# One layer of a hybrid decoder on one core: the second head's keys and queries loaded into the place of the first rows

## The chip, the core and the metric

The kernel runs on one core of a Trainium2 chip: TensorE for matrix products, VectorE, ScalarE and GpSimd for the rest, SyncE as the queue that issues nearly all DMAs. The metric is device time in microseconds of one execution.

## What is computed

2048 prompt rows and 32 sample rows of 1024 numbers are normed, and one projection gives all head groups and the gate:

```
h = rmsnorm(x); p = h @ w_in
cb, cc, ch, q, k, v, mq, z = split(p)               # 3x256, 3x512, 256, 1024 columns
conv_y = cb * conv3(cc * ch)
for win, dil in ((128,1), (512,4), (2048,16)):      # 8 heads x 64, ALiBi, causal band per residue class
    o, lse = softmax_band(q, k, v, win, dil)
attn_o = merge(outs, lses)                          # weights by the softmax denominators
mem_o = softmax(mq @ mk^T) @ mv                     # 4 heads x 64, 256 memory tokens
x = x + (concat(conv_y, attn_o, mem_o) * silu(z)) @ w_out
y = rmsnorm(x)
```

The sample rows attend to 8 caches of 2048 keys. Outputs are y of both kinds of rows, the windows of k and v, the conv buffer and the memory keys and values, all in float32.

## The kernel before, in words

**Rows and projections.** Products run with operands split into a high and a low part, three products each (`mm3`, L354). The normed rows lie column-wise in `hT`: half "A" (`hA_hi`, `hA_lo`) holds the first 1024 prompt rows and the 32 sample rows, half "B" the others. `proj_steps` (L383) takes one tile of 128 weight columns through column groups of rows: 384, 384 and 288 of A, 512 and 512 of B (`GROUPS`); each group is 24 matmuls into one PSUM bank, which is then evicted.

**z.** z has eight column tiles. `ev_z` (L680) applies SiLU on ScalarE into one of two buffers `ehi` and spills it to the DRAM tensor `dz` (`spill`, L374 to L377); prompt and sample columns of the last group of A are two spills. The last two tiles (`ZL` is 2) are projected for half B at their place, and for half A in `z_last` (L697), which `interleave` (L1104) mixes with the score products of head 0. Then the room of the rows is given up: `p0.close()`.

**Heads.** Eight attention heads, then four memory heads, are `units`. Odd units take their tiles from `vals[1]` and `keys[1]`, even ones from `vals[0]` and `keys[0]`. `load_qk` (L802 to L808) issues six DMAs of 512 KB by SyncE: high and low part of k into `ks`, and of q twice each into `qh` and `ql`. `regroup` (L823) copies `ks` into `kr` in another order, four copies on ScalarE for dilation 16 and later four for dilation 4. `scores` runs the products `qk` (L791, L792): those of dilation 16 by `kr`, those of dilation 1 by `ks`, those of dilation 4 by `kr`. `values` subtracts a running maximum (`Rm`, fetched through the DRAM tensor `dmax`, L747 and L748) on GpSimd, takes the exponential on ScalarE (L924, L925 for `S`, L929 for `S3`, L945 for `SS`), and multiplies with `v` (L917).

**What sets the order.** Head 1's pools lie in the room of the rows, so they are opened after `z_last`, and `units[1].load_qk()` (L1107) and its `regroup` come next. From then on `periods` (L1123) runs: the scores of unit n beside the values of unit n - 1, with the loads of unit n + 1 in it (`loads`, L1110); TensorE and SyncE keep the order in which the code issues there (`manual_schedule`), the other engines are ordered by a scheduler by priorities. Every engine works its own list in order. SyncE's DMAs use eight completion counters in turn, `DMAHW0` to `DMAHW7`; a DMA waits for the one before it on its counter. After the last memory head's scores the room of the keys is given up, and W_out is loaded in eight chunks, split into `woh` and `wol` in the pool `wo` (L1138 to L1152).

Of the kernel before, what the change touches and what calls it, by code (L numbers as in the profile page):

```python
# [9 lines left out]
R = mybir.dt.float32r  # L10
# [8 lines left out]
D = 1024  # L19
T = 2048  # L20
# [5 lines left out]
ZL = 2  # L26
# [248 lines left out]
def tile_step(ctx, tc, x_prompt, x_sample, mem_prompt, ck, cv, cconv, cmk, cmv, g_in, w_in, conv_w,  # L275
# [87 lines left out]
    NA = T // 2 + NS  # L363
    GROUPS = [("A", 0, 384), ("A", 384, 384), ("A", 768, 288), ("B", 0, 512), ("B", 512, 512)]
    hT = {}

    def split_cols(half, o, n):

        if half == "B":
            return [(0, 1024 + o, n)]  # L370
        if o + n <= 1024:
            return [(0, o, n)]
        return [(0, o, 1024 - o), (1024 - o, T, NS)]
# [9 lines left out]
    def proj_steps(src, c0, evac, halves, lo_eng, keep=None):  # L383

        wh, wl = keep.get(c0) or load_w(src, c0, lo_eng) if keep is not None else load_w(src, c0, lo_eng)
        if keep is not None:
            keep[c0] = wh, wl
        for half, o, n in GROUPS:
            if half not in halves:
                continue  # L390
            hh, hl = hT[half]
            ps = psP.tile([128, 512], F, name="pp")
            mm3(ps[:, :n], lambda d: wh[:, d], lambda d: wl[:, d], lambda d: hh[:, d, o:o + n], lambda d: hl[:, d, o:o + n])
            evac(ps[:, :n], half, o, n)
            yield

    xr = x_prompt[0].rearrange("(b r) d -> r b d", r=16)
# [15 lines left out]
    hA = p0.enter_context(tc.tile_pool(name="rowsA", bufs=1))  # L413
    wp = p0.enter_context(tc.tile_pool(name="weights", bufs=2))
    hT["A"] = [hA.tile([128, 8, NA], R, name="hA_" + s) for s in ("hi", "lo")]
    with ExitStack() as p1:
        hB = p1.enter_context(tc.tile_pool(name="rowsB", bufs=1, side="right"))
        hT["B"] = [hB.tile([128, 8, 1024], R, name="hB_" + s) for s in ("hi", "lo")]
        with ExitStack() as pv:
# [41 lines left out]
            def rows(rb):  # L461
# [3 lines left out]
                norm_t((xr[rb] if rb else None) if rb < 16 else xs, n, gt, hT[half], c0)  # L465
                return half, c0

            def values(rb, half, c0):
                if rb == 16:
                    c0 = NA - 128  # L470
                hh, hl = hT[half]
                ps = psP.tile([128, 512], F, name="pp")
                mm3(ps, lambda d: hh[:, d, c0:c0 + 128], lambda d: hl[:, d, c0:c0 + 128], lambda d: wvh[:, d], lambda d: wvl[:, d])
# [223 lines left out]
    def z_last():  # L697
        for ct in range(8 - ZL, 8):
            yield from z_proj(ct, "A")
# [8 lines left out]
    keys[0] = p2q.enter_context(tc.tile_pool(name="keys0", bufs=1, side="right", reuse_waits="tile"))  # L708

# [397 lines left out]
    keys[1] = p2q.enter_context(tc.tile_pool(name="keys1", bufs=1, reuse_waits="tile"))  # L1107
    units[1].load_qk()
# [31 lines left out]
    woh, wol = {}, {}  # L1140
    for d in reversed(CH):
        woh[d] = wo.tile([128, D], R, name="woh%d" % d)
        wol[d] = wo.tile([128, D], R, name="wol%d" % d)
# [151 lines left out]
```

## Time and profile before

| | |
|---|---|
| median of the timed runs | 1369.4 us (1365.25 to 1371.61, 3 runs) |
| profiled execution | 1372.67 us, span 1370.6 us |
| TensorE busy | 1241.9 us (91%), mean granted clock 0.961 |
| VectorE, ScalarE, GpSimd busy | 643.0, 436.6, 458.9 us |
| DMA | 229.56 MB, mean 167 GB/s |

The profiled execution's own time is the span, first to last instruction, and 2 us around it. Times below count from the span's start. The idle time of an engine is put down to what ended it; an instruction's own row shows it in brackets.

### The profile page before, as it was taken

Reading aid. Unit: us, or ns where it says so; the run is one execution under the profiler, and the core shown is the slowest. Engines: PE = TensorE matmul, PEld = TensorE weight load, DVE = VectorE, ACT = ScalarE, POOL = GpSimd, SP = SyncE. Lnnn points to the kernel's source line nnn. Section 1 sums busy time; section 2 is a strip of 40 time slices with the busy share of each in tenths; the row PEclk is TensorE's granted clock in tenths of the full one; section 3 lists DMA queues with packets and bytes.
Section 4 is the critical chain, followed back from the end, with each engine's and each line's share of the span. In section 5 each row is a group of like instructions: output and inputs, shape, how many; then the busy total and the mean of one; then the engine's idle time right before and its main releaser. Section 6 shows DMA issues by size and latency. Waiting matters only on the chain. (4 is left out here: it accounts for less than half of the span.)

```text
span 1370.6 us, 20158 instructions
## 1 busy us (share of the span) xinstructions
PE 1241.9 (91%) x7814; PEld 1000.6 (73%) x7814; DVE 643.0 (47%) x1201; ACT 436.6 (32%) x692; POOL 458.9 (33%) x398
## 2 busy tenths in 40 slices
PE   6999999988899999999999938889889877999997
PEld 5778898977788777778887936666667442678886
DVE  4555121466556612301640437777777235554442
ACT  5433032223232010011122225556665465421111
POOL 3120010355556201101640014666666565110000
PEclk9999999999999999999999969999999989999999
DMA  6453142477887246575546357888887846876641
GB/s 230 131 154 104 41 145 87 169 260 244 268 259 253 74 96 160 158 190 176 162 151 157 86 123 169 173 183 186 185 185 164 204 112 186 240 218 202 190 155 70
DMA packets 228102, 229.56 MB, mean 167 GB/s; under 512 B 67348, under 2 KB 182280, under 8 KB 223912
## 3 DMA queue, kind: packets, MB, share of 16 engines
q1 hardware_dynamic: 216488, 207.30, 55.9%
q10 hardware_dynamic: 11520, 20.98, 4.1%
q8 instruction: 62, 1.02, 0.3%
q14 instruction: 32, 0.26, 0.1%
HBM read 171.92 MB, written 56.31 MB: 167 GB/s over the span
## 5 line engine op out<-in xcount | busy, mean ns | idle before, releaser
L359 PE MATMUL b<-hA_hi,whi 128*128 128x384 f32 (+1 forms) x576 | 191.4, 332 | 13.7 <-ACT big L607 11.4
L359 PE MATMUL b<-hA_hi,wlo 128*128 128x384 f32 (+1 forms) x576 | 189.0, 328 | 0.0
L359 PE MATMUL b<-hA_lo,whi 128*128 128x384 f32 (+1 forms) x576 | 188.6, 327 | 0.0
L351 POOL TENSOR_TENSOR wlo<-wraw,whi 128x512 fp32r<-128x512 f32 x56 | 80.9, 1461 | 295.5 <-ACT whi L350 294.8
L359 PE MATMUL b<-hB_hi,whi 128*128 128x512 f32 (+1 forms) x416 | 164.1, 394 | 9.7 <-ACT big L607 2.0
L124 POOL TENSOR_TENSOR spr<-sk,sqb 128x512 f32<-128x512 f32 (+2 forms) x110 | 121.7, 1117 | 127.1 <-DMA sqb<-dqs 43.3
L359 PE MATMUL b<-hB_lo,whi 128*128 128x512 f32 (+1 forms) x416 | 163.1, 392 | 0.0
L359 PE MATMUL b<-hB_hi,wlo 128*128 128x512 f32 (+1 forms) x416 | 162.8, 391 | 0.0
L359 PEld LDWEIGHTS b<-hA_hi,whi 128*128 128x128 f32 x576 | 110.2, 191 | 20.0 <-ACT big L607 12.3
L125 DVE TENSOR_REDUCE sc<-spr 128x8 f32<-128x512 f32 (+1 forms) x160 | 88.4, 572 | 73.7 <-POOL spr L124 73.3
L795 DVE SCALAR_TENSOR_TENSOR S<-dt,b 128x128 f32<-128x128 f32 (+2 forms) x224 | 70.1, 355 | 103.6 <-PE b L792 69.7
L359 PEld LDWEIGHTS b<-hA_hi,wlo 128*128 128x128 f32 x576 | 110.1, 191 | 4.1 <-issue 3.3
L359 PEld LDWEIGHTS b<-hA_lo,whi 128*128 128x128 f32 x576 | 110.0, 191 | 2.9 <-issue 2.9
L1198 PE MATMUL b<-woh,mh 128*128 128x512 f32 x256 | 99.9, 393 | 5.0 <-DVE xo L1228 3.3
L409 POOL TENSOR_TENSOR ss<-ss,nhalf 128x1 f32<-128x1 f32 (+1 forms) x34 | 20.8, 613 | 243.9 <-DVE ss L408 235.0
L1198 PE MATMUL b<-woh,ml 128*128 128x512 f32 x256 | 100.4, 394 | 0.2 <-DVE ml L1190 0.2
L359 PEld LDWEIGHTS b<-hB_hi,whi 128*128 128x128 f32 x416 | 79.2, 190 | 28.1 <-issue 3.2
L1198 PE MATMUL b<-wol,mh 128*128 128x512 f32 x256 | 98.7, 389 | 0.0
L928 POOL TENSOR_TENSOR S<-S,Rm 128x512 f32<-128x512 f32 x32 | 40.3, 1281 | 170.3 <-DMA Rm<-dmax 146.4
L828 ACT ACTIVATE kr<-ks 128x512 fp32r<-128x512 f32 x64 | 69.0, 1117 | 79.8 <-PE b L792 63.8
L791 PE MATMUL b<-qh,kr 128*128 128x256 f32 x256 | 75.1, 323 | 21.4 <-DMA qh<-dq_hi 20.9
L359 PEld LDWEIGHTS b<-hB_lo,whi 128*128 128x128 f32 x416 | 79.2, 190 | 19.8 <-issue 3.3
(234 smaller groups left out, 2370.1 us busy)
## 6 DMA issues: line engine op xcount, KB each, us to landing
sk<-in_cache_win_k_dram SPq DMA_DIRECT2D x72, 256.0 KB, 4.1
vq<-in_cache_win_v_dram SPq DMA_DIRECT2D x36, 512.0 KB, 4.1
wraw<-in_w_in_dram SPq DMA_DIRECT2D x48, 256.0 KB, 3.7
sqb<-dqs SPq DMA_DIRECT2D x48, 256.0 KB, 4.3
qh<-dq_hi SPq DMA_DIRECT2D x24, 512.0 KB, 10.4
ql<-dq_lo SPq DMA_DIRECT2D x24, 512.0 KB, 10.6
Rm<-dmax SPq DMA_DIRECT2D x24, 512.0 KB, 4.4
v<-out_dram SPq DMA_DIRECT2D x16, 512.0 KB, 17.8
```

The costliest lines, as they stand in the source:

```text
L124: E.tensor_mul(pr[:n, :width], kt, qt)
L125: nc.vector.tensor_reduce(dst, pr[:n, :width].rearrange("p (h e) -> p h e", e=64), axis=AX.X, op=OP.add)
L351: lo_eng.tensor_sub(lo[:, a:a + 4], raw, f32(hi[:, a:a + 4]))
L359: nc.tensor.matmul(ps, a(d), b(d), start=(n == 0), stop=(n == 23))
L409: nc.gpsimd.tensor_tensor(ss[:n], ss[:n], nhalf[:n], op=OP.pow)
L791: nc.tensor.matmul(out, keys, a, start=True, stop=False)
L795: nc.vector.scalar_tensor_tensor(S, dt, sl, ps, op0=OP.mult, op1=OP.add)
L828: nc.scalar.activation(self.kr[:, r4 * 512:(r4 + 1) * 512].rearrange("p (a b) -> p a b", a=d // 4), src[:, r4], AF.Copy)
L928: nc.gpsimd.tensor_sub(S3[:, r4], S3[:, r4], mr[:, r4])
L1198: nc.tensor.matmul(self.ps[k], l[:, d], r[d][:, sl], start=first and i == 0, stop=last and i == 2)
```

## The change

Three things, all about half A's first group of 384 rows.

1. Half A is held in three tiles, one for each column group: `hA0`, `hA1`, `hA2`, each with both parts. `hA0` keeps its room to the end of the kernel; the two others are given up with the rest of the rows.
2. `z_last` goes by column group: the first group of both tiles of z, then the second of both, then the third. After the first group of both it calls `units[1].load_qk()`.
3. `ks`, `qh` and `ql` of all odd units are three parts of `hA0` (3 x 2048 = 2 x 8 x 384 elements of a partition). Only `kr` and the partial maxima come from the pool `keys1`, opened after `z_last` as before. At the end, chunks 0 to 2 of `woh` and `wol` lie in `hA0`.

```diff
--- before.py
+++ after.py
@@ -364,6 +364,13 @@
     GROUPS = [("A", 0, 384), ("A", 384, 384), ("A", 768, 288), ("B", 0, 512), ("B", 512, 512)]
     hT = {}
 
+    def rows_at(half, o):
+
+        if half == "B":
+            return hT["B"], o
+        g = min(o // 384, 2)
+        return (hT["A"][g][:, 0], hT["A"][g][:, 1]), o - 384 * g
+
     def split_cols(half, o, n):
 
         if half == "B":
@@ -388,9 +395,9 @@
         for half, o, n in GROUPS:
             if half not in halves:
                 continue
-            hh, hl = hT[half]
+            (hh, hl), p = rows_at(half, o)
             ps = psP.tile([128, 512], F, name="pp")
-            mm3(ps[:, :n], lambda d: wh[:, d], lambda d: wl[:, d], lambda d: hh[:, d, o:o + n], lambda d: hl[:, d, o:o + n])
+            mm3(ps[:, :n], lambda d: wh[:, d], lambda d: wl[:, d], lambda d: hh[:, d, p:p + n], lambda d: hl[:, d, p:p + n])
             evac(ps[:, :n], half, o, n)
             yield
 
@@ -410,9 +417,10 @@
         return ss
 
     p0 = ctx.enter_context(ExitStack())
-    hA = p0.enter_context(tc.tile_pool(name="rowsA", bufs=1))
+    hA = ctx.enter_context(tc.tile_pool(name="rowsA", bufs=1))
+    hA2 = p0.enter_context(tc.tile_pool(name="rowsA2", bufs=1))
     wp = p0.enter_context(tc.tile_pool(name="weights", bufs=2))
-    hT["A"] = [hA.tile([128, 8, NA], R, name="hA_" + s) for s in ("hi", "lo")]
+    hT["A"] = [(hA2 if i else hA).tile([128, 2, 8, n], R, name="hA%d" % i) for i, n in enumerate((384, 384, NA - 768))]
     with ExitStack() as p1:
         hB = p1.enter_context(tc.tile_pool(name="rowsB", bufs=1, side="right"))
         hT["B"] = [hB.tile([128, 8, 1024], R, name="hB_" + s) for s in ("hi", "lo")]
@@ -462,15 +470,16 @@
                 n = 128 if rb < 16 else NS
                 half = "B" if 8 <= rb < 16 else "A"
                 c0 = 1024 if rb == 16 else (rb % 8) * 128
-                norm_t((xr[rb] if rb else None) if rb < 16 else xs, n, gt, hT[half], c0)
+                hs, p = rows_at(half, c0)
+                norm_t((xr[rb] if rb else None) if rb < 16 else xs, n, gt, hs, p)
                 return half, c0
 
             def values(rb, half, c0):
                 if rb == 16:
                     c0 = NA - 128
-                hh, hl = hT[half]
+                (hh, hl), p = rows_at(half, c0)
                 ps = psP.tile([128, 512], F, name="pp")
-                mm3(ps, lambda d: hh[:, d, c0:c0 + 128], lambda d: hl[:, d, c0:c0 + 128], lambda d: wvh[:, d], lambda d: wvl[:, d])
+                mm3(ps, lambda d: hh[:, d, p:p + 128], lambda d: hl[:, d, p:p + 128], lambda d: wvh[:, d], lambda d: wvl[:, d])
                 vt = wk.tile([128, 512], F, name="vt", bufs=1)
                 if rb < 16:
                     nc.vector.tensor_copy(vt, ps)
@@ -695,8 +704,13 @@
 
 
     def z_last():
-        for ct in range(8 - ZL, 8):
-            yield from z_proj(ct, "A")
+        steps = [z_proj(ct, "A") for ct in range(8 - ZL, 8)]
+        for g in range(3):
+            for x in steps:
+                next(x)
+                yield
+            if g == 0:
+                units[1].load_qk()
 
 
     p2 = ctx.enter_context(ExitStack())
@@ -706,6 +720,16 @@
     p2q = ctx.enter_context(ExitStack())
     vals[0] = p2v.enter_context(tc.tile_pool(name="vals0", bufs=1, side="right", reuse_waits="tile"))
     keys[0] = p2q.enter_context(tc.tile_pool(name="keys0", bufs=1, side="right", reuse_waits="tile"))
+
+    class Keys1:
+
+
+        def tile(self, shape, dtype, name=None):
+            if name in ("ks", "qh", "ql"):
+                i = ("ks", "qh", "ql").index(name)
+                return hT["A"][0].rearrange("p s c n -> p (s c n)")[:, T * i:T * i + T]
+            return self.pool.tile(shape, dtype, name=name)
+    keys[1] = Keys1()
 
 
     d1 = dt1.rearrange("p (r J c) -> p r J c", r=4, J=2)
@@ -1104,8 +1128,7 @@
     interleave(units[0].scores(), z_last(), 24, 3 * ZL)
     p0.close()
     vals[1] = ctx.enter_context(tc.tile_pool(name="vals1", bufs=1, reuse_waits="tile"))
-    keys[1] = p2q.enter_context(tc.tile_pool(name="keys1", bufs=1, reuse_waits="tile"))
-    units[1].load_qk()
+    keys[1].pool = p2q.enter_context(tc.tile_pool(name="keys1", bufs=1, reuse_waits="tile"))
     units[1].regroup(16, range(4))
 
     def loads(n):
@@ -1138,9 +1161,11 @@
     wo = ctx.enter_context(tc.tile_pool(name="wo", bufs=1, reuse_waits="tile"))
     CH = range(8)
     woh, wol = {}, {}
+
+    room = [hT["A"][0].rearrange("p s c n -> p (s c n)")[:, D * i:D * i + D] for i in range(6)]
     for d in reversed(CH):
-        woh[d] = wo.tile([128, D], R, name="woh%d" % d)
-        wol[d] = wo.tile([128, D], R, name="wol%d" % d)
+        woh[d] = room.pop() if d < 3 else wo.tile([128, D], R, name="woh%d" % d)
+        wol[d] = room.pop() if d < 3 else wo.tile([128, D], R, name="wol%d" % d)
 
     def load_wo():
         for d in CH:
```

The number of instructions is the same on every engine. Line numbers after the change are up to 24 higher: L384 is the spill, L830 to L831 and L741 to L742 the loads, L852 `regroup`.

SyncE's list at the end of z, before the change. `ehi_6360`, `6416`, `6476` are the three groups of the seventh z tile, `6534`, `6592`, `6652` of the eighth; `ks_6698`, `qh_6701`, `ql_6702` are head 1's:

```order
L377 DMA dz_72<-ehi_6360 128x384 [waits DMAHW1_49,Activation_49]
L377 DMA dz_72<-ehi_6416 128x384 [waits DMAHW2_49,Activation_49]
L377 DMA dz_72<-ehi_6476 128x256 [waits DMAHW3_49,Activation_49]
L377 DMA dz_72<-ehi_6476 128x32 [waits DMAHW4_49]
L377 DMA dz_72<-ehi_6534 128x384 [waits DMAHW5_49,Activation_49]
L377 DMA dz_72<-ehi_6592 128x384 [waits DMAHW6_49,Activation_49]
L377 DMA dz_72<-ehi_6652 128x256 [waits DMAHW7_49,Activation_49]
L747 DMA dmax0_6298<-mc_6676 32x32 [waits DMAHW0_49,DVE_49]
L377 DMA dz_72<-ehi_6652 128x32 [waits DMAHW1_49]
L748 DMA Rm_6323<-dmax0_6298 128x1024 [waits DMAHW2_49,DMAHW0_49]
L806 DMA ks_6698<-dk_hi_68 64x2048 [waits DMAHW3_49,PE_49,Pool_49]
L807 DMA ks_6698<-dk_lo_69 64x2048 [waits DMAHW4_49]
```

SyncE's list there after the change. `ehi_6364` and `ehi_6420` are the first groups of the two tiles, `6486` and `6543` the second, `6601` and `6662` the third:

```order
L384 DMA dz_72<-ehi_6364 128x384 [waits DMAHW1_49,Activation_49]
L830 DMA hA0_98<-dk_hi_68 64x2048 [waits DMAHW2_49,PE_49]
L831 DMA hA0_98<-dk_lo_69 64x2048 [waits DMAHW3_49]
L741 DMA hA0_98<-dq_hi_66 64x2048 [waits DMAHW4_49,PE_49]
L742 DMA hA0_98<-dq_lo_67 64x2048 [waits DMAHW5_49,PE_49]
L384 DMA dz_72<-ehi_6420 128x384 [waits DMAHW6_49,Activation_49]
L741 DMA hA0_98<-dq_hi_66 64x2048 [waits DMAHW7_49]
L742 DMA hA0_98<-dq_lo_67 64x2048 [waits DMAHW0_49]
L384 DMA dz_72<-ehi_6486 128x384 [waits DMAHW1_49,Activation_49]
L384 DMA dz_72<-ehi_6543 128x384 [waits DMAHW2_49,Activation_49]
L384 DMA dz_72<-ehi_6601 128x256 [waits DMAHW3_49,Activation_49]
L384 DMA dz_72<-ehi_6601 128x32 [waits DMAHW4_49]
```

The six loads stood behind all spills, `dmax` and `Rm`; now four stand behind the first spill, and the second spill is between them and the last two. The first of them waits for TensorE and its own counter. The two spills of `6662` come next, on counters 5 and 7 with `dmax` between them on 6, and then `Rm`. The spills from `6543` on wait for counters that loads have used.

ScalarE's list from the last eviction of z to the first copies of head 1's keys, before:

```order
L682 ACTIVATE ehi_6652<-b1_6627 128x288 [waits DMAHW5_49,PE_49,Activation_49]
L929 ACT_TABLE_LOAD [waits DVE_49]
L929 ACTIVATE S3_6324<-S3_6324 128x1024 [waits Pool_49]
L828 ACTIVATE kr_6707<-ks_6698 128x512 [waits DMAHW4_49,DMAHW6_49,DMAHW3_49,DMAHW7_49,DMAHW1_49,Activation_49]
L828 ACTIVATE kr_6707<-ks_6698 128x512 x3
```

and after, from the eviction of `ehi_6543`:

```order
L691 ACTIVATE ehi_6543<-b1_6518 128x384 [waits DMAHW6_49,PE_49,Activation_49]
L691 ACTIVATE ehi_6601<-b0_6576 128x288 [waits DMAHW1_49,PE_49,Activation_49]
L691 ACTIVATE ehi_6662<-b1_6637 128x288 [waits DMAHW2_49,PE_49,Activation_49]
L852 ACTIVATE kr_6708<-hA0_98 128x512 [waits DMAHW4_49,DMAHW5_49,DMAHW3_49,DMAHW7_49,Activation_49,Pool_49]
L852 ACTIVATE kr_6708<-hA0_98 128x512 x3
```

Before, a table load and an exponential of head 0 stand between the last eviction and the copies; now the copies follow the eviction. Their first one waits for counters 3, 4, 5 and 7, which in SyncE's list are last those of the spills of the third groups.

ScalarE's list around the copies for head 2 (`kr_6943<-ks_6799`) and the exponentials of head 0's second half (`S3`, then `S_6620` and `S_6665`), before:

```order
L828 ACTIVATE kr_6707<-ks_6698 128x512 [waits PE_49,Activation_49] x4
L929 ACTIVATE S3_6324<-S3_6324 128x1024 [waits Pool_49]
L828 ACTIVATE kr_6943<-ks_6799 128x512 [waits DMAHW4_49,DMAHW3_49]
L828 ACTIVATE kr_6943<-ks_6799 128x512 x3
L925 ACTIVATE S_6620<-S_6620 128x128 [waits Pool_49]
L924 ACTIVATE S_6620<-S_6620 128x768 [waits Pool_49]
L925 ACTIVATE S_6665<-S_6665 128x128 [waits Pool_49]
L924 ACTIVATE S_6665<-S_6665 128x768 [waits Pool_49]
```

and after, where these are `kr_6944<-ks_6800`, `S_6630` and `S_6675`:

```order
L852 ACTIVATE kr_6708<-hA0_98 128x512 [waits PE_49,Activation_49]
L948 ACTIVATE S_6569<-S_6569 128x768 [waits Pool_49]
L949 ACTIVATE S_6614<-S_6614 128x128 [waits Pool_49]
L948 ACTIVATE S_6614<-S_6614 128x768 [waits Pool_49]
L852 ACTIVATE kr_6944<-ks_6800 128x512 [waits DMAHW4_49,DMAHW3_49]
L852 ACTIVATE kr_6944<-ks_6800 128x512 x3
L953 ACTIVATE S3_6328<-S3_6328 128x1024 [waits Pool_49]
L949 ACTIVATE S_6630<-S_6630 128x128 [waits Pool_49]
L948 ACTIVATE S_6630<-S_6630 128x768 [waits Pool_49]
L949 ACTIVATE S_6675<-S_6675 128x128 [waits Pool_49]
```

The copies for head 2 stood behind the exponential of `S3` and now stand ahead of it.

## Rows read from the trace of the kernel before

**Rows 1.** The page's groups of instructions: busy, mean ns, idle before, its releaser.

```profile
L359 PE MATMUL b<-hA_hi,whi 128*128 128x384 f32 (+1 forms) x576 | 191.4, 332 | 13.7 <-ACT big L607 11.4
...
L791 PE MATMUL b<-qh,kr 128*128 128x256 f32 x256 | 75.1, 323 | 21.4 <-DMA qh<-dq_hi 20.9
```

**Rows 2.** Windows: span, each engine's busy time and instructions, clock, DMA share, GB/s.

```profile
733.29:750.89 17.60, 15.63 (x67) 12.38 (x65) 0.00 (x0) 6.16 (x8) 2.85 (x3) 0.96 0.96 224
770.00:798.60 28.60, 28.60 (x201) 28.36 (x199) 22.49 (x48) 5.42 (x8) 0.00 (x0) 1.00 0.28 65
798.60:819.84 21.24, 0.56 (x2) 0.29 (x2) 1.74 (x5) 8.54 (x11) 6.84 (x6) 0.55 0.76 180
819.84:852.27 32.43, 28.94 (x263) 22.13 (x265) 23.78 (x55) 15.63 (x18) 16.55 (x14) 0.88 0.79 163
852.27:888.19 35.92, 31.19 (x350) 23.93 (x346) 26.98 (x63) 20.99 (x27) 23.47 (x20) 0.95 0.81 177
```

**Rows 3.** TensorE's timeline around the gap: start, length, line, out<-in, [idle before <-releaser].

```profile
798.31 0.29 PE L359 MATMUL b<-hA_lo,whi 128*128 128x288 f32 x1
817.51 0.55 PE L791 MATMUL b<-qh,kr 128*128 128x256 f32 x1 [18.91 <-DMA qh<-dq_hi]
819.84 0.58 PE L792 MATMUL b<-ql,kr 128*128 128x256 f32 x1 [1.77 <-DMA ql<-dq_lo]
...
840.54 0.65 PE L917 MATMUL acc<-S,v 128*64 128x256 f32 x2 [1.71 <-ACT S L924]
```

**Rows 4.** SyncE's timeline, the same columns: issues of DMAs, head 0's loads first.

```profile
733.29 0.53 SPq L806 DMA_DIRECT2D ks<-dk_hi  x1
...
737.59 0.66 SPq L718 DMA_DIRECT2D ql<-dq_lo  x1
...
772.43 27.02 SPq L377 DMA_DIRECT2D dz<-ehi  x7
799.54 0.38 SPq L747 DMA_DIRECT2D dmax<-mc  x1
799.98 0.41 SPq L377 DMA_DIRECT2D dz<-ehi  x1
...
801.42 0.48 SPq L806 DMA_DIRECT2D ks<-dk_hi  x1
...
825.04 0.45 SPq L806 DMA_DIRECT2D ks<-dk_hi  x1
```

**Rows 5.** ScalarE's timeline, the same columns: evictions of z, copies, exponentials.

```profile
693.52 0.49 ACT L682 ACTIVATE ehi<-b 128x384 f32<-128x384 f32 x1 [3.84 <-DMA dz<-ehi]
...
776.71 0.49 ACT L682 ACTIVATE ehi<-b 128x384 f32<-128x384 f32 x1 [0.78 <-PE b L359]
...
793.52 0.49 ACT L682 ACTIVATE ehi<-b 128x384 f32<-128x384 f32 x1 [6.09 <-PE b L359]
798.69 0.41 ACT L682 ACTIVATE ehi<-b 128x288 f32<-128x288 f32 x1 [4.68 <-PE b L359]
...
810.42 3.92 ACT L828 ACTIVATE kr<-ks 128x512 fp32r<-128x512 f32 x4 [1.70 <-DMA ks<-dk_lo]
...
832.08 1.06 ACT L929 ACTIVATE S<-S 128x1024 f32<-128x1024 f32 x1 [4.11 <-POOL S L928]
835.49 4.07 ACT L828 ACTIVATE kr<-ks 128x512 fp32r<-128x512 f32 x4 [2.35 <-DMA ks<-dk_lo]
...
840.59 0.83 ACT L924 ACTIVATE S<-S 128x768 f32<-128x768 f32 x1
```

**Rows 6.** DMA issues of two short windows: KB each, us from issue to landing.

```profile
ql<-dq_lo SPq DMA_DIRECT2D x1, 512.0 KB, 13.3
...
dz<-ehi SPq DMA_DIRECT2D x1, 16.0 KB, 1.5
```

**Rows 7.** Timelines of TensorE and ScalarE where W_out's copies begin.

```profile
1145.40 0.40 PE L792 MATMUL b<-ql,ks 128*128 128x512 f32 x1
...
1155.37 0.63 ACT L1151 ACTIVATE woh<-woraw 128x512 fp32r<-128x512 f32 x1 [3.11 <-DMA woraw<-in_w_out_dram]
```

## The prediction, made before the changed kernel was run

> **What bounds the kernel now.** I read the page first, then the windows around the one long gap, then the timelines of TensorE, SyncE and ScalarE in that gap. On the page the products of the first attention stage, `qh` by `kr`, have 21.4 us of idle time ahead of them, nearly all put down to the DMA `qh<-dq_hi` [rows 1]. TensorE is busy for nine tenths of the span, so a gap of this size is a place and not a habit, and the windows find it [rows 2]: from 770.0 to 798.6 TensorE is busy for every microsecond at a granted clock of 1.00; in the next 21.24 us it is busy for 0.56; then head 1's period starts and lasts 32.43 us, and head 2's lasts 35.92. TensorE's timeline shows the edges [rows 3]: the last product of z at 798.31, then 18.91 us of waiting for `qh` and, after one product, 1.77 us for `ql`, until 819.84. SyncE's timeline tells why [rows 4]: seven spills of z hold that queue from 772.43 on, then come `dmax`, the last spill of z, `Rm`, and only at 801.42 the first of head 1's six loads of 512 KB. They can't come sooner, since the room they are put into is that of the rows which z still reads. So what is late in this place is 3 MB that are asked for after z instead of beside it.
>
> **How long these loads take beside z.** Head 0's own six loads show it: first issue 733.29, last issue 737.59 and 13.3 us more to land, 750.89, so 17.6 us [rows 4, 6]. In that stretch TensorE was busy for 15.63 of 17.60 us with other projections [rows 2]; a full TensorE did not slow them, nor they it. In the gap itself the same six took from 801.42 to 819.84, 18.4 us at most. In the window of z, the DMA engines are busy for 0.28 of the time [rows 2].
>
> **The change, part by part.**
>
> The rows in three tiles: the same products in the same number and, until the last z columns, the same order. Cost: none. A finer tile could also let a product of the first half start sooner; all waits ahead of those products together are 13.7 us, and most are for another operand, `big` [rows 1]. Bounds 0 and 13.7; I take 0, since no instruction before the last z columns moves.
>
> The last z columns by groups: six groups as before, 384, 384, 384, 384, 288, 288 columns instead of 384, 384, 288 twice. Same columns, same weights, so the end of z stays at 798.6. What changes is when the first 384 rows are read for the last time: at the second group. The second eviction of z in the old order starts at 776.71, after 0.78 us of waiting for TensorE [rows 5]; the second group of the new order is as wide, so the tile is free at about 776.3.
>
> The loads moved: in the new order of SyncE they stand behind the first spill. From 776.3 they take 17.6 to 18.4 us and land at 794 to 795, some 4 us before z ends. The stall for `qh` and `ql`, 18.91 + 1.77 = 20.7 us, goes. They are moved past six spills of z, `dmax` and `Rm`, which stand behind them. ScalarE's evictions share two buffers, so each waits for the spill two before it. The spill that decides is the third (`ehi_6486`): issued behind all six loads, it may land at about 796, and the fifth eviction, due near 793.5 [rows 5], waits for it some 2 us. That frees a PSUM bank 2 us late; the sixth group of z uses the other bank, so TensorE feels nothing, and the last eviction stays at 798.69 [rows 5]. Such a wait on a spill is in the trace: 3.84 us ahead of an eviction at 693.52 [rows 5].
>
> The Trainium skill, page "DMA: Bandwidth & Descriptors", section "Queues, rings and completion order", says that on each DMA engine the descriptors of one issuing queue are consumed in ring order. By it the spills do stand behind the whole 3 MB, as I took it above; were they to share the engines instead, the third spill would be out in a few microseconds and the 2 us would not be there either. The sum is the same by both; the rule speaks for the last rival below, and the row at 693.52 agrees that spills hold evictions up.
>
> What is late next: head 1's keys still have to be regrouped by ScalarE, four copies `kr<-ks`, 3.92 us for the four [rows 5], and the first product needs the first of them, about 1.0. `kr` lies over the two buffers that z is spilled from, so in the order of ScalarE its first copy waits for the last spills, the last of them the 16 KB at 799.98 which land in 1.5 us [rows 4, 6]: 801.5. First product 802.7 with the hops; before it was 819.84 with both operands. That is 17.1 us, not 20.7. Were that wait absent, the copies could start at 799.1 and the product at 800.2, 19.6 us sooner.
>
> Head 1's period: the work is the same, but on ScalarE the four copies for head 2 now stand ahead of the exponentials of head 0's second half; before they stood behind `S3`'s. Behind them in that queue are the exponentials `S`, and TensorE's products with `v` wait for those. Head 2's loads are issued 5.2 us after the first product (825.04 against 819.84 [rows 3, 4]), so now at about 807.9. The copies started 10.45 us after that issue (835.49 [rows 5]), so 818.3, or about 817 if the queue is less full. They end at 821 to 822.4, then come the exponential of `S3`, 1.06, and a small and a large one of `S`, the large one 0.83 [rows 5], so 823 to 824.6. TensorE came to these products 19.0 us after the first one of the head (840.54 less a wait of 1.71 [rows 3]), so now at 821.7 with less warm-up, say 820 to 821. It waits 3.7 to 5.0, less the 1.71 of before: 2.0 to 3.3 lost. Bounds: nothing lost, if TensorE gets there no sooner than the exponentials, and 3.5 + 5.0 = 8.5, if the period also grows to the 35.92 of the next one [rows 2]. I take 2.5, from the rows of this very period.
>
> W_out partly in the first tile: the same copies and products. The last scores, whose keys lie there, are done at 1145.8, and the first copy of W_out starts at 1155.37, 3.11 us of it waiting for its own load [rows 7]. The room is free ten microseconds before it is written. Some copies of chunk 3 move behind others; by the length of two or three copies of 0.6, plus or minus 2 us. I take 0.
>
> **The sum.** 17.1 - 2.5 = 14.6 us. The profiled execution took 1372.67 us for its span of 1370.6; less 14.6 it would be 1358.1. It lies 3.3 us above the median of the timed runs, 1369.4; the same 14.6 from there is 1354.8.
>
> **Rivals.**
> - All of it is kept. Head 1's period loses nothing, and its start no longer runs cold. After the gap the clock is 0.88 over the period against 0.95 in the next [rows 2]; 7% of 32.4 us is up to 2.3. With the 17.1 that is 17 to 19.4 us: 1350 to 1352, I say 1351. For it: the clock of 0.55 belongs to a gap of 21 us [rows 2], and one of 4 is left. Against it: the order of the copies on ScalarE.
> - Half is given back in head 1's period, by the upper bound there: 17.1 - 8.5 = 8.6, 1361; 5 to 10 us by what of it meets. For it: head 2's period is 3.5 us longer than head 1's and has the order that head 1 gets now. Against: nothing else in it changes.
> - It doesn't do what it says: the loads wait for something that ends with z. Then 1369. For it: tiles in borrowed room have hidden waits. Against: in the order the first load waits for a count of TensorE and of its own completion counter alone, and if that count were the end of z, the spill that stands behind the loads would hold up the evictions and z could not end.
> - Slower: the spills of z stand behind 3 MB. If the loads take long, the third spill lands late, the fifth eviction and with it the sixth and the last spill and the first copy `kr` move by the same. From a landing of the loads at about 796 each microsecond costs one: the 14.6 are used up when they land at 810.6, 34.3 us after 776.3, and from 818 on, 41 us after it, the kernel is slower by more than 0.5%. For it: the row at 693.52. Against: 17.6 us beside a busy TensorE [rows 2, 4, 6]. It would come out at 1377 or more.
>
> **How the numbers follow.** The forecast has 58%, all kept 20%, half given back 12%, no effect 5%, slower 5%. 0.5% is 6.8 us, about what a measurement of this kernel can tell from no change. Faster by more: 58 + 20 + two thirds of 12, 86%; within: 4 + 5, 9%; slower 5%. The range takes in the all-kept case with 4 us below it and half given back: 1347 to 1362. The forecast's own range is 1351 to 1358.
>
> **What would show it.** In the profile after, head 1's `ks`, `qh`, `ql` are issued from about 776.5 on while z runs; TensorE's gap at the end of z is 4 us, ended by ScalarE's `kr`, not by a DMA; the next `dmax` of a period stands near 838 instead of 852.27; ahead of the products `acc<-S,v` of that period a wait of 4 to 5 us for ScalarE. It is wrong if the gap stays 20 us with another releaser, if waits for PSUM or evictions appear inside z before 798, or if the period after the gap is over 38 us.

## The result, and the profile after

The changed kernel takes 1363.96 us, median of 15 runs (1354.07 to 1371.46), beside 1371.61 for the kernel before in 15 runs on the same chip: ratio 0.994, 95% interval 0.9922 to 0.9959. By the ratio it is faster by 8.2 us (0.6% of 1371.61) where 14.6 were forecast, and its time lies 2 us above the range. The profiled execution took 1366.68 us, with a span of 1364.5. Ratios leave out two executions further on, of 1422 and 1727 us, that ran at a much lower granted clock; medians contain them.

The windows of the changed kernel, with the columns of [rows 2], over the stages shown there and, in the last two rows, from the first `dmax` of the last pair to the first output product, and the 97 us after that (the `dmax` come in pairs, one pair for each of the twelve heads):

```profile
770.00:798.72 28.72, 28.72 (x205) 28.72 (x203) 22.24 (x47) 5.54 (x8) 0.00 (x0) 1.00 0.81 180
798.72:803.09 4.37, 0.29 (x3) 0.05 (x1) 2.03 (x6) 1.52 (x3) 0.00 (x0) 0.92 0.25 71
803.09:836.93 33.84, 28.82 (x264) 22.68 (x266) 23.80 (x55) 22.28 (x27) 23.49 (x20) 0.86 0.82 167
...
1131.67:1152.65 20.98, 12.01 (x54) 3.22 (x50) 13.14 (x13) 9.24 (x14) 11.88 (x5) 0.92 0.88 265
1152.65:1249.66 97.01, 92.30 (x388) 70.69 (x389) 50.38 (x62) 27.43 (x42) 8.60 (x10) 0.96 0.68 205
```

The same two last stages of the kernel before, which the prediction did not look at:

```profile
1146.90:1165.82 18.92, 11.91 (x53) 3.59 (x49) 10.86 (x13) 9.24 (x14) 11.06 (x5) 0.91 0.94 268
1165.82:1258.05 92.23, 88.40 (x389) 68.62 (x390) 50.45 (x62) 27.77 (x42) 11.38 (x11) 1.00 0.74 220
```

From the start of z's last product to the first product of head 1 it was 21.5 us (798.31 to 819.84 [rows 3]) and is now 4.37. The DMA engines are busy for 0.81 of z's last stretch instead of 0.28, and TensorE is still busy in every microsecond of it at a granted clock of 1.00: the loads beside z cost z nothing. The loss is in the last two rows. The stretch ahead of the first output product takes 20.98 instead of 18.92 us, and nearly the same number of matmuls (388 against 389) takes 97.01 instead of 92.23, at a clock of 0.96 instead of 1.00.

TensorE's timeline of the changed kernel (start, length, line, names, idle before and releaser) around the gap, at the products with `v` of head 1's period, and among the first output products:

```profile
798.72 0.29 PE L359 MATMUL b<-hA,whi 128*128 128x288 f32 x1
803.09 0.58 PE L815 MATMUL b<-hA,kr 128*128 128x256 f32 x1 [4.08 <-ACT kr L852]
...
823.19 1.98 PE L941 MATMUL acc<-S,v 128*64 128x128 f32 x16 [4.04 <-ACT S L953]
...
1152.65 0.73 PE L1223 MATMUL b<-hA,mh 128*128 128x512 f32 x2 [3.91 <-ACT mh L1214]
...
1187.86 1.07 PE L1223 MATMUL b<-hA,mh 128*128 128x512 f32 x2 [4.40 <-ACT mh L1214]
```

They answer to [rows 3] and [rows 7]. The 18.91 us for `qh` are gone and 4.08 for `kr` stand in their place. The products that wait 4.04 read the exponential of `S3`; before, the same sixteen waited for nothing, and the wait of 1.71 was that of a later group, which now has none. The two counterparts, before and then after:

```profile
835.60 1.09 PE L917 MATMUL acc<-S,v 128*64 128x128 f32 x16
```

```profile
827.78 1.73 PE L941 MATMUL acc<-S,v 128*64 128x256 f32 x16
```

The last row of the changed kernel's timeline has no partner before: nothing of that size is to be found in the output products there.

SyncE's timeline, against [rows 4]; and two of its spills by the DMA issues (KB each, us to landing), against [rows 6]: the one ahead of the loads, and the first behind all six:

```profile
772.87 0.34 SPq L384 DMA_DIRECT2D dz<-ehi  x1
775.37 0.48 SPq L830 DMA_DIRECT2D hA<-dk_hi  x1
...
779.38 0.59 SPq L742 DMA_DIRECT2D hA<-dq_lo  x1
783.28 16.58 SPq L384 DMA_DIRECT2D dz<-ehi  x5
```

```profile
dz<-ehi SPq DMA_DIRECT2D x1, 192.0 KB, 2.9
...
dz<-ehi SPq DMA_DIRECT2D x1, 192.0 KB, 10.1
```

The loads are issued at 775.37 instead of 801.42. The spill issued at 783.28, behind all six, lands 10.1 us later, at 793.4. ScalarE's timeline, against [rows 5], shows that this is early enough:

```profile
793.92 0.41 ACT L691 ACTIVATE ehi<-b 128x288 f32<-128x288 f32 x1 [4.09 <-PE b L359]
799.10 0.41 ACT L691 ACTIVATE ehi<-b 128x288 f32<-128x288 f32 x1 [4.77 <-PE b L359]
801.98 5.03 ACT L852 ACTIVATE kr<-hA 128x512 fp32r<-128x512 f32 x5 [2.47 <-DMA dz<-ehi]
...
818.18 4.01 ACT L852 ACTIVATE kr<-ks 128x512 fp32r<-128x512 f32 x4 [3.53 <-DMA ks<-dk_lo]
822.10 1.04 ACT L953 ACTIVATE S<-S 128x1024 f32<-128x1024 f32 x1
```

The fifth and sixth evictions wait for TensorE alone; the first copy of `kr` waits 2.47 us for the last spill; head 2's copies start at 818.18, ahead of the exponential of `S3`.

One execution of each of the two kernels, stage by stage (us): end of z 798.31 and 798.72; gap 21.5 and 4.4; from there to the second pair's first `dmax` 32.4 and 33.8; to the seventh pair's 176.9 and 175.6; to the last pair's 117.8 and 119.2; to the first output product 18.9 and 21.0; to the end 204.8 and 211.8. Up to the last pair's first `dmax` the changed kernel is 15.2 us ahead. The gap gives 17.1; the last two stages take back 9.1 of it. An execution picked from many scatters by some 4 us, so what follows leans on stages that repeat from profile to profile, and on ratios.

### The profile page after: what moved, and what is told of

It is laid out like the page before. It is cut to its first block, busy times and chain, and to the rows that moved or that the text cites. A ratio compares the mean times of both kernels' runs of the same rounds, so it can differ in the third digit from the quotient of the medians.

```text
span 1364.5 us, 20164 instructions
## 1 busy us (share of the span) xinstructions
PE 1245.4 (91%) x7814; PEld 1003.5 (74%) x7814; DVE 646.2 (47%) x1201; ACT 435.9 (32%) x692; POOL 457.7 (34%) x398
## 3 DMA queue, kind: packets, MB, share of 16 engines
q10 hardware_dynamic: 11520, 20.98, 4.1%
## 5 line engine op out<-in xcount | busy, mean ns | idle before, releaser
L359 PE MATMUL b<-hA,whi 128*128 128x384 f32 (+1 forms) x1152 | 290.8, 331 | 19.9 <-ACT big L616 12.4
L359 PEld LDWEIGHTS b<-hA,whi 128*128 128x128 f32 x1152 | 208.2, 194 | 29.0 <-ACT big L616 13.5
L359 PE MATMUL b<-hA,wlo 128*128 128x384 f32 (+1 forms) x576 | 189.6, 329 | 0.0
L359 PEld LDWEIGHTS b<-hA,wlo 128*128 128x128 f32 x576 | 111.7, 194 | 4.1 <-issue 3.3
L416 POOL TENSOR_TENSOR ss<-ss,nhalf 128x1 f32<-128x1 f32 (+1 forms) x34 | 19.6, 578 | 251.1 <-DVE ss L415 251.1
L359 PEld LDWEIGHTS b<-hB_hi,wlo 128*128 128x128 f32 x416 | 78.9, 190 | 18.1 <-issue 2.5
L761 DVE TRANSPOSE_TENSOR_REDUCE mparts<-S 128x12 f32<-128x384 f32 (+1 forms) x96 | 76.4, 824 | 25.4 <-ACT S L1050 25.3
L1223 PE MATMUL b<-hA,mh 128*128 128x512 f32 x192 | 67.2, 409 | 8.3 <-ACT mh L1214 8.3
L350 ACT ACTIVATE whi<-wraw 128x512 fp32r<-128x512 f32 x56 | 32.9, 625 | 107.1 <-PE b L359 102.8
L1223 PE MATMUL b<-woh,mh 128*128 128x512 f32 x160 | 63.4, 397 | 0.0
L1223 PE MATMUL b<-woh,ml 128*128 128x512 f32 x160 | 63.3, 397 | 0.0
```

What stands on the lines that cost most here:

```text
L359: nc.tensor.matmul(ps, a(d), b(d), start=(n == 0), stop=(n == 23))
L761: nc.vector.tensor_reduce(out, scores, axis=AX.X, op=OP.max, apply_transpose=True)
L1223: nc.tensor.matmul(self.ps[k], l[:, d], r[d][:, sl], start=first and i == 0, stop=last and i == 2)
```

## The experiments

The tail is what lies between the last pair's first `dmax` and the end; in it the output products multiply row blocks of 128 rows by W_out. A row block ("row 2" for short) is loaded into `mx`, multiplied there by the gate on VectorE, and split: `mh`, a copy by ScalarE, is the high part of the operand, and `ml`, a subtraction on VectorE, the low part. There were three theories of the tail's loss. The products: TensorE's list there has another order, two products of row 2 ahead of row 1's remaining 46. The lists: loads, copies and subtractions of W_out stand elsewhere in those of SyncE, ScalarE and VectorE. The loads: that they come early costs something further on.

**after2**: the changed kernel once more.

> The changed kernel again, unchanged, with a new profile. In its first profile head 1 starts 16 us sooner, and the last 6 us of that is all that is left at the end: 4.4 us go in one wait of TensorE between the first output rows, for row block 2's operand, and after that wait the output products follow each other every 233.3 ns instead of 228.9. Theory, the order of the products does it: the same wait of 4 to 5 us again, and the ratio to the kernel before 0.992 to 0.996. Rival, a mishap of one execution: no such wait here, a ratio near 0.989. The spacing of 233.3 ns is either bound to that wait (again 233) or to the execution (then another value).

1364.17 us, ratio 0.9933 (0.9904 to 0.9962). Gap 4.4; from the last pair's first `dmax` to the end 231.3 us (before: 223.7). The wait among the first output products is there again, 4.80 us. TensorE's windows of this run (span, busy time, clock, DMA share, GB/s):

```profile
1186.50:1191.50 5.00, 3.29 (x8) 0.50 0.52 136
1196.50:1201.50 5.00, 5.00 (x23) 1.00 1.01 319
```

After the wait TensorE runs at its lower level of 1.2 GHz for some microseconds: the loss is more than the wait.

**rows_in_order**: TensorE keeps the written order in the output products, row 1's before row 2's.

```diff
-    for r in early:
-        for _ in r.products(CH[7:]):
-    ...
+    with tc.manual_schedule(engines={mybir.EngineType.PE}):
+        for r in early:
+            for _ in r.products(CH[7:]):
+    ...
```

> The changed kernel with TensorE's order held from the last chunk of the early row blocks on, so that row block 1's 48 products come ahead of row block 2's first two, as in the kernel before. Nothing else moves but one addition on VectorE. Theory, these two products are what takes the gain back: the wait of 4.4 us goes, with the cold products behind it some 6 us, and up to 3 more if the slower spacing goes with it; 1364 less 6 to 9, so 1355 to 1358, a ratio of 0.988 to 0.990. Rival, the loss lies in the room and the copies of W_out: the wait moves a few products on and the ratio stays at 0.994.

1366.93 us, 0.9942 (0.9915 to 0.9968), no better than after2. The waits of TensorE in this stretch (in total, times, longest):

```profile
PE b L1223 <- DVE ml L1215: 5.4, 1, 5.4
```

The wait moved to row 1's first product with the low part `ml`, which VectorE makes, and grew. So the products theory falls: TensorE's order alone is not the cause. Why `ml` comes late is to be seen under tail_order_kept.

**loads_late**: the groups of the last z columns in the order second, third, first, so that the tile of the first rows is free only at the end of z. The loads go there, but late.

```diff
-        steps = [z_proj(ct, "A") for ct in range(8 - ZL, 8)]
+        steps = [z_proj(ct, "A", GROUPS[1:3] + GROUPS[:1]) for ct in range(8 - ZL, 8)]
 ...
-            if g == 0:
+            if g == 2:
```

> The changed kernel with the column groups of the last z tiles in the order second, third, first, so that the first tile of rows is free only at the end of z and head 1's loads start there, at 798.6 or a little later; everything behind it as in the changed kernel. Theory, the early loads give 16 us and the tail loses 8 to 10 on its own: TensorE's gap is back at 17 to 19 us and the time is that of the kernel before plus 5 to 9, a ratio of 1.004 to 1.007. Rival, the tail loses because everything comes earlier: then the tail loses nothing here, and the ratio is 0.998 to 1.001.

1374.14 us, 1.0006 (0.998 to 1.0032). TensorE's timeline at the end of z:

```profile
813.43 0.55 PE L815 MATMUL b<-hA,kr 128*128 128x256 f32 x1 [12.40 <-DMA hA<-dq_hi]
815.88 0.55 PE L816 MATMUL b<-hA,kr 128*128 128x256 f32 x1 [1.89 <-DMA hA<-dq_lo]
```

The gap is 15.8 us, ended by DMAs as before. It is shorter than 21.5 because nothing but the tile holds the loads now: they are issued 1.8 us ahead of z's last product (798.29 against 800.11), before 3.1 us after it. The ratio is the one that the rival gave, but not for the rival's reason: with the early loads gone, the tail still takes 230.4 us with a wait of 4.79, and what makes the time shorter than the theory's is the gap. So the early loads are not the cause of the tail's loss. Between this run and after2 lie 0.73%, 10 us: what loading beside z is worth, for a difference of 11.4 us in the gap.

**z_by_tile**: the old order, each column's three groups together, with the loads behind the first group of the last column.

```diff
-        for g in range(3):
-            for x in steps:
+        for x in steps:
+            for g in range(3):
                 next(x)
                 yield
-            if g == 0:
-                units[1].load_qk()
+                if x is steps[1] and g == 0:
+                    units[1].load_qk()
```

> The changed kernel with the last z tiles in their old order, tile by tile; head 1's loads go out after the first group of the second tile, at 787 instead of 775. Theory, the copies kr wait for the last spill of z and cover most of the loads: ks has landed at 795, qh and ql at 805, so TensorE's gap ends near 805 instead of 803, ended by a DMA, and the time is 2 us over that of the changed kernel, a ratio of 0.994 to 0.997. Rival, the group order is needed: the loads share the engines with the spills and land at 810 or later, a gap of 12 us and a ratio of 1.000.

1368.78 us, 0.9967 (0.9944 to 0.999): half of the gain. TensorE and then ScalarE at the end of z:

```profile
809.77 0.58 PE L815 MATMUL b<-hA,kr 128*128 128x256 f32 x1 [6.49 <-ACT kr L852]
```

```profile
808.66 4.01 ACT L852 ACTIVATE kr<-hA 128x512 fp32r<-128x512 f32 x4 [4.88 <-DMA dz<-ehi]
```

The loads are issued at 790.35, 15 us later than in the changed kernel. They are in before they are asked for, but the last spills stand behind them and land late, and the first copy of `kr` waits for those for 4.88 us instead of 2.47. This is the last rival's mechanism, at a small price. The gap is 2.4 us longer than after2's and the time, by the ratios, 4.7 us (0.34%); the other 2 us are not explained, since its tail is shorter (227.1), and the intervals of the two overlap.

**tail_order_kept**: the changed kernel with a higher priority for loading, copying and subtracting the chunks 3 and 7 of W_out. The rooms stay. The lists of all engines from there on become those of before, but for one subtraction on VectorE.

```diff
+                with tc.high_priority(400 if d in (3, 7) else 0):
                     nc.sync.dma_start(raw, w_out[0][d * 128:(d + 1) * 128, sl])
                     nc.scalar.activation(woh[d][:, sl], raw, AF.Copy)
                     (nc.gpsimd if ... else nc.vector).tensor_sub(wol[d][:, sl], raw, f32(woh[d][:, sl]))
```

> The changed kernel with a higher priority for the loads, copies and subtractions of chunks 3 and 7 of W_out; by that alone the lists of all engines from there to the end are those of the kernel before, while the first chunks still lie in the first tile of rows. The last row of the runs so far: TensorE runs dry for 4.4 to 5.4 us in the first output rows in every kernel with the new order, and also where row block 1's products stood first; from the last memory head's first dmax to the end it is 227 to 233 us there and 224 in the kernel before. Theory, the order of W_out's loads and copies costs that: the wait goes, first output product 19 us after that dmax and the end 224 us after it, 5 to 7 us less than the changed kernel, a ratio to the kernel before of 0.987 to 0.990. Rival, it is the room (chunks in the first tile, more traffic there): the wait stays and the ratio is 0.993 to 0.995.

1360.08 us, 0.9898 (0.9868 to 0.9927). SyncE's timelines at the last loads of W_out, of the changed kernel and of the kernel before:

```profile
1156.04 12.80 SPq L1175 DMA_DIRECT2D woraw<-in_w_out_dram  x6
1170.41 1.26 SPq L812 DMA_DIRECT2D dmix<-osb  x2
1171.76 2.08 SPq L1175 DMA_DIRECT2D woraw<-in_w_out_dram  x2
```

```profile
1171.15 10.05 SPq L1150 DMA_DIRECT2D woraw<-in_w_out_dram  x8
1184.95 1.26 SPq L788 DMA_DIRECT2D dmix<-osb  x2
```

In the changed kernel the last head's stores `dmix<-osb` stand ahead of chunk 7's two loads and hold SyncE from 1168.84 to 1171.76. Before, and here too, all eight loads go first. The stores are not the wait that ends last, though: behind them the two loads wait another 1.4 us for VectorE's subtractions, which free their buffers. ScalarE's timelines of the changed kernel and of the kernel before:

```profile
1181.72 1.15 ACT L1214 ACTIVATE mh<-mx 128x896 fp32r<-128x896 f32 x2 [3.65 <-PE b L1223]
```

```profile
1191.90 1.15 ACT L1189 ACTIVATE mh<-mx 128x896 fp32r<-128x896 f32 x2 [1.27 <-PE b L1198]
```

With the loads, chunk 7's copies come 4 to 5 us later after the first output product than in the others, the products that read them end later, and the copy `mh<-mx` of row 1 waits 3.65 us for their buffer instead of 1.27. TensorE loses nothing by that: it has products without a break until 1183.46, and by 1182.87 that copy is done. Only then it waits, for 4.40 us, as its waits over the output products (changed, then tail_order_kept: total, times, longest) show:

```profile
PE b L1223 <- ACT mh L1214: 8.3, 2, 4.4
```

```profile
PE b L1224 <- ACT mh L1215: 2.7, 1, 2.7
```

What it waits for stands in VectorE's timelines, of the changed kernel, of the kernel before and of this one:

```profile
1185.41 1.23 DVE L1211 TENSOR_TENSOR mx<-mx,zg 128x1024 f32<-128x1024 f32 x1 [3.01 <-DMA mx<-dmix]
...
1187.15 1.08 DVE L1215 TENSOR_TENSOR ml<-mx,mh 128x896 fp32r<-128x896 f32 x1
```

```profile
1192.88 1.29 DVE L1190 TENSOR_TENSOR ml<-mx,mh 128x896 fp32r<-128x896 f32 x2 [0.21 <-ACT mh L1189]
...
1199.14 1.23 DVE L1186 TENSOR_TENSOR mx<-mx,zg 128x1024 f32<-128x1024 f32 x1 [3.44 <-DMA mx<-dmix]
```

```profile
1181.91 1.29 DVE L1216 TENSOR_TENSOR ml<-mx,mh 128x896 fp32r<-128x896 f32 x2
...
1187.72 1.23 DVE L1212 TENSOR_TENSOR mx<-mx,zg 128x1024 f32<-128x1024 f32 x1 [2.99 <-DMA mx<-dmix]
```

In the changed kernel VectorE has row 2's `mx` ahead of row 1's `ml`. The `mx` waits for its load, and the `ml` waits with it, until 1187.15, though its `mh` was there at 1182.87. TensorE's list has the same order: the product at 1187.86 is row 2's, whose copy to `mh` runs from 1186.75 to 1187.81, and row 1's products with `ml` stand behind it. In the other two kernels `ml` follows its copy at once, and while row 2's `mx` waits about 3 us for the same load, TensorE has row 1's products to do. The six profiles with the new lists all have this order on VectorE and a wait of 4.4 to 5.4 us. The seven with the old lists have the other order and no wait over 2.0 us behind the first output product. In rows_in_order, where only TensorE's list was put back, TensorE waited for this very `ml`.

With the old order the long wait is gone, and from the first output product to the end it takes 204.6 us (before 204.8). The theory of the lists stands, and the wait itself is traced to VectorE's list; no run changed that list alone. The stretch ahead of the first output product stays 20.8 us long, where 19 were expected.

**kr_free**: the same, and the last z groups of both columns are evicted to the two buffers of the raw weights (`wraw`), with a pad of 4 KB ahead of `kr`, so that its first copy has no spill of these groups to wait for.

```diff
-            zt = zw.tile([128, 512], F, name="ehi")
+            if half == "A" and o == 768 and ct >= 8 - ZL:
+                zt = wp.tile([128, 4, 128], F, name="wraw").rearrange("p a n -> p (a n)")
+            else:
+                zt = zw.tile([128, 512], F, name="ehi")
 ...
+    keys[1].pool.tile([128, 1024], F, name="pad")
```

> As tail_order_kept, and the last two groups of z are evicted into the two buffers of the raw weights, with kr 4 KB further up in its pool, so that kr's first copy waits for no spill of the last groups. Theory, the 4.1 us that TensorE waits for kr are eviction, last spill and copy in a row: without the spill the copy starts at 0.3 us after the end of z instead of 3.2, the gap is 1.5 to 2 us and the time 2 to 3 us under tail_order_kept, a ratio of 0.985 to 0.988. Rival, the next operand takes its place (S3's room, a PSUM bank): gap 3 us or more, no difference that shows.

1357.4 us, 0.9884 (0.9856 to 0.9912). TensorE and ScalarE at the end of z:

```profile
800.43 0.39 PE L818 MATMUL b<-hA,kr 128*128 128x256 f32 x1 [1.51 <-ACT kr L855]
```

```profile
799.32 6.08 ACT L855 ACTIVATE kr<-hA 128x512 fp32r<-128x512 f32 x6
```

No copy waits for a spill any more and the gap is 1.8 us. The gap gives 19.7 us against the kernel before, where the prediction had 19.6 for the case without that wait. The time misses its range, 0.985 to 0.988, by a little: it is 1.9 us under tail_order_kept.

**late_tail_kept**: loads_late and tail_order_kept together.

> As loads_late (head 1's loads at the end of z), with the order from W_out on as in the kernel before. What is left of the change is the split and the rooms. Theory, these cost nothing by themselves: the gap after z is 14 to 16 us against 21 in the kernel before, all else equal, so 5 to 6 us faster than before, a ratio of 0.995 to 0.997, and 5 to 7 us under loads_late. Rival, the rooms cost 5 us or more: 0.999 to 1.002.

1371.64 us, 0.9982 (0.9961 to 1.0003). The gap is 15.7 us, as expected. Against loads_late, on another chip, the ratio is 0.24% less, in the direction of the lists theory, but the interval holds 1 as well as the expected values: inconclusive by itself. The long wait is gone here too, the largest being 3.1 us ahead of the first output product; yet the tail takes 228.2 us, 2.8 more than in tail_order_kept, which is not explained.

**before_again, after3, tail_kept2, kr_free2**: the kernel before against itself, and the three versions side by side on one chip.

> The kernel before, unchanged, for a second profile. Theory: 224 us from the last memory head's first dmax to the end, no wait over 2.5 us of TensorE in the output rows, a gap of 21 us after z. Rival, the tail of the first profile was a lucky one: 228 us or more, with waits of 4 us. Ratio 1.

> The changed kernel once more, beside the next two on one chip. Both theories: 0.993 to 0.994, and a wait of 4 to 5 us of TensorE in the output rows.

> tail_order_kept again, beside the changed kernel on one chip. Theory, the order of W_out's loads and copies costs the changed kernel 5 us: 4 to 7 us under after3, a ratio of 0.988 to 0.991. Rival, the difference between 0.9935 and 0.9898 was that of two chips: within 2 us of after3.

> kr_free again, the fastest so far. Theory, the gap after z is 1.8 us instead of 4.4: 2 to 3 us under tail_kept2, a ratio of 0.986 to 0.989. Rival, what the gap loses comes back in head 1's period: no difference to tail_kept2.

| kernel | us | ratio | 95% interval | last pair's `dmax` to first output product, to end |
|---|---|---|---|---|
| before_again | 1374.2 | 1.0003 | 0.9976 to 1.0029 | 18.8, 204.2 |
| after3 | 1366.35 | 0.9931 | 0.9906 to 0.9956 | 21.0, 209.9 |
| tail_kept2 | 1365.23 | 0.9911 | 0.9886 to 0.9936 | 21.0, 203.6 |
| kr_free2 | 1361.89 | 0.9899 | 0.9866 to 0.9931 | 20.9, 205.9 |

The order is the same as in the first round, with smaller steps: the tail's order is worth 2.7 us by these ratios, where 4 to 7 were expected, and 4.8 by the first (0.9933 less 0.9898, from two chips); `kr` freed, 1.6 and 1.9, where 2 to 3 were expected. The intervals of neighbours overlap, so each step by itself is seen in the profile rather than in the time. By the ratios the two versions with the old tail order are the fastest that ran, and kr_free is the version to keep: 14 to 16 us below the kernel before.

## Why the prediction was half right

The loads hidden: right. Issue 775.37 (forecast 776.3). The spill behind the last load was in at 793.4 (the loads: 794 to 795), and no load is waited for at the end of z. Cost to z: none, as forecast.

Spills behind the loads: right in the order, wrong in the consequence. The third spill needed 10.1 us, where one of the same size ahead of the loads needed 2.9; it landed at 793.4 instead of 796, and so the fifth eviction did not wait the 2 us. The Trainium skill, page "DMA: Bandwidth & Descriptors", section "Queues, rings and completion order", has descriptors of one ring consumed in order; by that, the spill's 10.1 us are the 3 MB ahead of it. The trace agrees with it here, and in z_by_tile, where the last spills hold the copy up for 4.88 us.

The new wait, `kr` for the last spill: right. Copy at 801.98 (801.5), product at 803.09 (802.7), gap 4.37; gain in the gap 17.1 as forecast. kr_free shows that it was this wait.

Head 1's period: right in the cause that was named and near in size, but by other products, which is part luck. The prediction expected the wait at the products that stand 19.0 us behind the head's first one and read the large exponentials of `S`. Those wait for nothing now. The wait of 4.04 us is at the sixteen products ahead of them, which read the exponential of `S3`: that one had been done before the copies and now comes behind them. The waits of before, 1.71 and 0.29 us, are gone, so the net loss at this point is 2.0 us (forecast 2.5). The forecast of the wait, 3.7 to 5.0, doesn't follow from its own times either: 823 to 824.6 less 820 to 821 is 2.0 to 4.6, and 0.3 to 2.9 less the 1.71. The period is 33.84 us instead of 32.43, and 33.6 to 35.3 in five other profiles with this order and early loads; before_again has 29.6, so its length is known to 3 us only. That the order of copies and exponentials does this is read from the timelines; it was not tried by itself.

W_out in the first tile: this is the step that failed. "[...] by the length of two or three copies of 0.6, plus or minus 2 us. I take 0." It is 2.1 us ahead of the first output product and 3.4 to 7 after it. The prediction looked at when the room is free and when the first copy starts, took the moved copies at their own length, and took the rest for "the same copies and products". It did not read the lists behind the copies. There row 2's `mx`, which waits for a load, had come ahead of row 1's `ml` on VectorE, and TensorE waits 4.4 to 5.4 us for what stands behind it and then goes on at its lower clock. Since the scheduler wrote all lists anew, they could have been compared to the end of the program before any run, as was done at the end of z. The range missed for the same reason: the bound of 2 was a multiple of an instruction's length, not the length of a wait. All that the prediction named as signs came out (the loads beside z, a gap of 4 us ended by `kr`, the next `dmax` at 836.93, a wait of 4 us for ScalarE), and none of them lies in the tail.

The base moved too: 1371.61 in these runs, where the forecast started from 1369.4. From there the same 8.2 us would give 1361.2, within the range; the gain falls short of 14.6 all the same.

The rival "half is given back" gave the nearest time, 1361, but puts the loss in head 1's period, where there is little of it. The rival "all of it is kept" had the start of that period no longer cold; it is cold after a gap of 4.4 us too, with a clock of 0.86 over the period (before: 0.88).

Open: why the scheduler chose another order in the tail (it does so also with the loads late), and the 2.1 us ahead of the first output product. There VectorE has a third subtraction behind the pair of `osb`, and its work beside GpSimd's subtractions is slow, in the changed kernel on VectorE and then on GpSimd:

```profile
1146.15 2.87 DVE L1177 TENSOR_TENSOR hA<-woraw,hA 128x512 fp32r<-128x512 f32 x1
1148.95 2.56 DVE L1211 TENSOR_TENSOR mx<-mx,zg 128x256 f32<-128x256 f32 x1
```

```profile
1146.13 5.09 POOL L1067 TENSOR_TENSOR S<-S,Rm 128x1024 f32<-128x1024 f32 x2
```

Before, `mx` took 1.39 at this place. z_by_tile has the same rooms and the same order on VectorE, but there the subtraction took 0.68 and `mx` 1.92, and the stretch is 18.9 us long, as before. So neither the rooms nor this order cost the 2.1 us by themselves; that it is how the work of the two engines falls together is likely, and rests on one profile. A version without the third subtraction was not tried.

## What to carry to other kernels

When a change gives tiles other rooms, compare the lists of every engine to the end of the program, not only where the edit is: a step that has come to stand behind one that waits for a load waits as long as that load, and so does whoever needs it. Price such a move by the wait of the instruction ahead of it, not by the step's own length. When a wait shows, ask what stood ahead of the instruction that ended it, and follow that to the wait that ended last, before blaming the first thing that has moved. And a load taken into a busy stretch is free only if what is issued behind it in the same queue isn't needed soon.

## What the runs showed of the hardware

TensorE goes on at another clock level after a gap of 4.4 us (the changed kernel) than after one of 1.8 (kr_free). The stretches from the first product of head 1 on, with the columns of TensorE's windows above:

```profile
803.09:805.59 2.50, 2.50 (x11) 0.50 0.43 146
805.59:808.09 2.50, 2.50 (x14) 0.50 0.01 2
808.09:810.59 2.50, 2.50 (x17) 0.78 0.60 167
```

```profile
800.43:802.93 2.50, 2.50 (x20) 1.00 0.37 91
802.93:805.43 2.50, 1.59 (x13) 1.00 0.43 162
```

The first goes on at 1.2 GHz for some 6 us, as the kernel before does after its gap of 21 us (a clock of 0.50 and 0.58 in the first two stretches of 2.5 us from 819.84); the second at 2.4 GHz throughout, and kr_free2 likewise. Head 1's period is 32.3 us in kr_free (34.9 in kr_free2, 33.8 after).

The output products of the one execution profiled as the changed kernel stand 233.3 ns apart from the wait on, at a granted clock of 1.00, and 228.9 on average in each of the others. That is some 3 us of its 211.8, and the reason why it is the longest; no run explains it.

A subtraction of 128x512 on VectorE that began 0.09 us before GpSimd's of 128x1024 took 0.68 us in z_by_tile (their rows below); the one shown above began 0.02 us after GpSimd's, and took 2.87.

```profile
1150.79 0.68 DVE L1177 TENSOR_TENSOR hA<-woraw,hA 128x512 fp32r<-128x512 f32 x1
```

```profile
1150.88 5.30 POOL L1067 TENSOR_TENSOR S<-S,Rm 128x1024 f32<-128x1024 f32 x2
```
